# The results of attention kept in four tiles instead of one, and the temporaries of the first key and value chunks put into memory that is not yet in use

## The chip, the cores and the metric

The kernel runs on one core of a Trainium2 chip. A core has a matrix engine (PE; PEld is its weight load), three engines for elementwise work (DVE, ACT, POOL) and a queue engine (SP) that issues all of this kernel's transfers. Each engine runs its instructions in the order in which they stand in its queue, and waits on semaphores for the others. The metric is the time of one execution in microseconds (us) on the device, as the median of several runs: 1191.7 us before the change (1190.87 to 1192.7, three runs).

## The reference

One layer of a decoder, for a prompt of 1024 tokens and for 8 sequences of 8 new tokens each ("sample" tokens, 64 in all, kept as tile 8 beside the prompt's tiles 0 to 7 of 128 tokens). All in float32, model width 1024.

```
mixer:  h = LN0(x)*(1+scale1)+shift1 ; [q|k|v|zu|zv] = h @ w_in
        group A: chunked causal spatial gating unit  u * (tril(W_s) v + b_s)
        group B: sliding-window (128) GQA with per-head sinks, partial rotary
        x = LN1(alpha*x + gate1 * concat(A, B) @ w_o)
ffn:    h = LN0(x)*(1+scale2)+shift2 ; x = LN2(alpha*x + gate2 * SwiGLU(h))
```

Group B has 8 query heads of width 64, which share 2 key and value heads. Keys and queries are rotated (the first 16 of 64 features), and a block of 128 queries sees its own and the previous block of keys. The outputs are both token sets, the new key and value windows, and the normalised v rows of the gating unit.

## The kernel before, in words

Products of float32 are made as three products of split operands (high times high, low times high, high times low), so every weight is loaded as a raw tile and split: ACT copies the high part (`load_unit`, L104) and DVE subtracts it for the low part (L105). The pair is called a unit; units go into the four places of the pool `wts` or into places of a pool that the caller names.

The stages of the mixer, in the program's order:

1. Normalisation and the u and zv projections (token-major products, L212 for prompt tiles and L216 for tile 8), with the gating unit's small products (L408), which DVE multiplies into the u tiles (L414). The u tiles are stored to a scratch tensor (L419).
2. Projections of keys, values and queries (`project`, L496), in three chunks of tokens: c = 0 and 1 of 384, c = 2 of 320. A key or query chunk is then rotated (`rotate`): DVE shuffles it out of PSUM into `sh` (L505), ACT copies it into `z` (L506), POOL does three elementwise operations on them (`pool_tt`, L109). The rotated keys are copied and split into `KS` (L531 to L536). A value chunk is copied into `v32` (L548), transposed (L552) and split into `VS`. Products of this stage go into the two PSUM banks of tag a (the third key chunk into one of tag c), so a new chunk waits until DVE and ACT have read the one two before it.
3. Attention: for each pair of query heads t = 0 to 3 and each pair of token blocks, scores (L627), softmax (L596 to L614, for part of the blocks on POOL, L109 `s<-s,den`), transposes (L643), copies and splits of these (L645, L646), the product with values (L651), and the sum of its two halves by DVE into `stash` (L655, L657). For t = 3 the pairs go in the order (6,7), (0,1), (2,3), (4,5). After each of these `split_attention` splits two tiles of `stash` into the operand of the output projection (ACT L449, DVE L450). Attention of the sample tokens (`attend_sample`) lies between, with the cached keys and values `KC` and `VC`.
4. The output projection with units `wo[0]` to `wo[7]`, 128 rows of `w_o` each. `wo[4]` to `wo[7]` (the gating unit's rows) are made during attention in `wts`; `wo[0]` to `wo[3]` (attention's rows) after it, in the pool `w3`. `out_group(2)` does tiles 6, 7 and 8 (48 products L212 with `wo[0]` to `wo[3]` for tiles 6 and 7, whose other half `mix_part` has made earlier and stored, and 32 products L216 for tile 8), into all banks of tags a, b and d. `out_tile` then does tiles 0 to 5, 48 products each, in the banks a and b by turns. `prep_tile` brings the gating unit's results (load `mt`, transposes L458, L461, L462). `merge_tile` and `norm_tile` add the residual and normalise; for tiles 6 and 7 POOL does part of it (L109 `r<-r,g1p` and `r<-r,xt`), before which DVE can't read the bank (L838).
5. The feed-forward part: features (`ffn_features`, L880 to L906), which are stored and loaded again, and then a long run of products that keeps PE busy.

The order on each engine is not that of the source. The framework schedules the whole program when it is built, and decides by modelled times and by what waits for what, memory included: a tile that takes the memory of an earlier one waits for the last users of that one (`reuse_waits="tile"`: of the tiles that overlap it). So a change of places moves instructions.

The places on the right side of memory, in KiB per partition from the right end: `xb` 24 (it holds the x tiles at first, then rotation tables `rc` and `rs`, `KC`, `VC`, masks, the sample queries `QZ`, attention's half sum `o2s`), then `stash` 16. When both pools close, the same places go to `XF` (6) and then to the four units of `w3` (8 each, at 6 to 38), so these lie over `xb` and over `stash`. `sh` and `z` are tiles of the pool `rt` on the left side, in places that stage 1 used.

```
stash = stp.tile([P, 4, SEQ], F32, name="stash")
w3 = w3_ctx.enter_context(tc.tile_pool(name="w3", bufs=4, side="right", reuse_waits="tile"))
```

Of the kernel before, what the change touches and what calls it, by code (L numbers as in the profile page):

```python
# [10 lines left out]
F32 = mybir.dt.float32  # L11
# [6 lines left out]
P = 128  # L18
D = 1024
KD = D // P  # L20
SEQ = 1024
NS = 64
NTOK = SEQ + NS
# [22 lines left out]
def tile_block(  # L46
# [8 lines left out]
    nc = tc.nc  # L55
# [169 lines left out]
    st_ctx = ExitStack()  # L225
    xbp = st_ctx.enter_context(tc.tile_pool(name="xb", bufs=1, side="right"))
    xb = xbp.tile([P, 6 * D], F32, name="xb")

    offs = np.cumsum([0, NTOK, NTOK, 8 * P, 8 * P, 3 * P, 384, 512, 512, P])
    rc, rs, KC, VC, msk, msks, QZ, o2s, kvo = [xb[:, offs[n] : offs[n + 1]] for n in range(9)]  # L230
# [7 lines left out]
    with ExitStack() as p1:  # L238
# [8 lines left out]
        xt = [xb[:, i * D : (i + 1) * D] for i in range(6)]  # L247
# [124 lines left out]
        nc.sync.dma_start(out=KC, in_=kc_t)  # L372
        nc.sync.dma_start(out=VC, in_=vc_t)
# [68 lines left out]
    stp = st_ctx.enter_context(tc.tile_pool(name="stash", bufs=1, side="right", reuse_waits="tile"))  # L442
    stash = stp.tile([P, 4, SEQ], F32, name="stash")
    def split_attention(i):
        rows = rows_of(i)
        c, off = tok_cols(i)
        hi, lo = mix_dst(i, 0)
        sv = stash[:, :, i * P : i * P + rows] if i < 8 else ssm
        nc.scalar.activation(out=hi, in_=sv, func=AF.Copy)  # L449
        nc.vector.tensor_tensor(out=lo, in0=sv, in1=hi.bitcast(F32), op=ALU.subtract)  # L450
# [13 lines left out]
    with ExitStack() as p2:  # L464
# [22 lines left out]
        nc.gpsimd.memset(QZ, 0.0)  # L487

# [11 lines left out]
        def rotate(pt, c):  # L500
            n = CW[c]
            t0 = 384 * c
            sh = rt.tile([P, 384], F32, tag="sh", name="sh")
            z = rt.tile([P, 384], F32, tag="z", name="z")
# [18 lines left out]
        for c in range(3):  # L523
            z = rotate(project(units[0], c, "aac"[c]), c)
# [18 lines left out]

        units.append(load_unit(w_qkv[4]))
        for c in range(3):
            pt = project(units[1], c)
            v32 = rt.tile([P, 384], F32, tag="z", name="v32")
# [16 lines left out]

        units.append(load_unit(w_qkv[5]))
# [51 lines left out]
        def attend(t, bs):  # L617
# [38 lines left out]
            for h in range(2):  # L656
                nc.vector.tensor_tensor(  # L657
                    out=stash[64 * h : 64 * h + 64, t, bs[0] * P : (bs[0] + 2) * P].rearrange("p (b q) -> p b q", q=P),
# [48 lines left out]
        def load_wo(k, pool=None):  # L707
            wo[k] = load_unit(w_o[k * P : (k + 1) * P, :], pool)
# [64 lines left out]
    with ExitStack() as p3:  # L773
        w3_ctx = p3.enter_context(ExitStack())
        w3 = w3_ctx.enter_context(tc.tile_pool(name="w3", bufs=4, side="right", reuse_waits="tile"))
# [5 lines left out]
        for k in range(4):  # L781
            load_wo(k, w3)
# [761 lines left out]
```

## Time and profile before

| what | value |
|---|---|
| runs before | 1192.7, 1191.7, 1190.87 us; median 1191.7 us |
| the profiled execution | 1190.98 us, its span on the core 1189.2 us |
| busy share of the span | PE 95%, PEld 77%, DVE 67%, ACT 42%, POOL 14% |
| granted PE clock, mean | 0.979 of full speed |
| bytes moved | 204.96 MB, mean 172 GB/s |

A row of a timeline names the start and the length of a group, the engine, the line, output and inputs with their sizes, and in square brackets how long the engine stood idle before it and what ended that. Rows of matmuls have modelled ends. A row of a table by stretches has, for each stretch of the span, busy time and count of instructions per engine, the mean granted PE clock, and the share and rate of the transfers.

### The profile page before, as it was taken

The numbers are of one execution on the slowest core, as the hardware profiler recorded it, in microseconds if no ns is written. First come the engines' busy times: TensorE is split into PE (matmuls) and PEld (weight loads), VectorE is DVE, ScalarE is ACT, GpSimd is POOL, SyncE is SP. The second block draws the span as 40 slices with busy tenths as digits, with TensorE's granted clock in tenths as the row PEclk, the third lists the DMA queues.
The fourth block names the chain that finished last, engine by engine and source line by source line (L and its number), as shares of the span: only waits on it lengthen the run. The fifth ranks groups of instructions, "written<-read, shape, count | busy, mean of one in ns | idle before, by whom it ended". The sixth has DMA issues, their size and how long they took to land.

```text
span 1189.2 us, 16244 instructions
## 1 busy us (share of the span) xinstructions
PE 1126.9 (95%) x5845; PEld 914.7 (77%) x5845; DVE 801.2 (67%) x1460; ACT 505.3 (42%) x920; POOL 171.1 (14%) x173
## 2 busy tenths in 40 slices
PE   4999998999979999799999999999999999999997
PEld 2676688887758877477888888888888888788885
DVE  4434355898776979568487467467467565879786
ACT  3553124675761255545444434434433454343200
POOL 2212434654135111000000000000000000000021
PEclk9999998999989999799999999999999999999999
DMA  9935344122353424554545515515514488957951
GB/s 330 296 109 188 96 148 154 56 76 94 107 194 119 152 100 168 181 175 139 202 161 195 203 47 193 204 54 186 203 52 170 151 313 290 336 193 258 325 204 71
DMA packets 96352, 204.96 MB, mean 172 GB/s; under 512 B 10304, under 2 KB 32704, under 8 KB 96256
## 3 DMA queue, kind: packets, MB, share of 16 engines
q1 hardware_dynamic: 96272, 203.92, 49.6%
q8 instruction: 46, 0.75, 0.3%
q14 instruction: 34, 0.28, 0.1%
HBM read 149.43 MB, written 55.44 MB: 172 GB/s over the span
## 4 chain that ended last, share of the span: by engine, by line
PE 76%; DVE 10%; DMA 7%; ACT 3%; issue 2%; SPq 1%; POOL 1%; DVEq 0%; ACTq 0%; POOLq 0%
PE ps_a L967 17%; PE ps_b L967 13%; PE ps_a L212 11%; PE ps_b L212 4%; PE ps_c L973 3%; PE ps_a L1243 3%; PE ps_b L1243 3%; PE ps_c L1243 3%; PE ps_d L1243 3%; DMA g<-g_d 2%; PE ps_a L496 2%; DMA rwd<-in_w_down 1%; PE ps_d L364 1%; DVE s L614 1%; DVE bn L115 1%
## 5 line engine op out<-in xcount | busy, mean ns | idle before, releaser
L967 PE MATMUL ps_a<-H,wgu 128*128 128x512 f32 x560 | 160.1, 390 | 1.3 <-ACT wgu L956 1.3
L967 PEld LDWEIGHTS ps_a<-H,wgu 128*128 128x128 f32 x560 | 105.1, 188 | 23.7 <-ACT wgu L956 1.7
L957 DVE TENSOR_TENSOR wgu<-rawgu,wgu 128x1024 fp32r<-128x1024 f32 x79 | 96.2, 1220 | 33.1 <-ACT wgu L956 33.0
L1280 POOL TENSOR_TENSOR rstd<-ve,neghalf 128x1 f32<-128x1 f32 (+1 forms) x9 | 13.6, 1513 | 695.1 <-DVE ve L1278 695.1
L212 PE MATMUL ps_a<-unit,XA 128*128 128x512 f32 x384 | 103.9, 413 | 6.5 <-ACT unit L104 4.7
L956 ACT ACTIVATE wgu<-rawgu 128x1024 fp32r<-128x1024 f32 x79 | 82.0, 1055 | 58.4 <-PE ps_a L967 48.0
L967 PE MATMUL ps_b<-H,wgu 128*128 128x512 f32 x320 | 104.1, 390 | 0.0
L967 PE MATMUL ps_b<-XA,wgu 128*128 128x512 f32 x344 | 96.6, 396 | 0.0
L212 PEld LDWEIGHTS ps_a<-unit,XA 128*128 128x128 f32 x384 | 73.2, 196 | 28.0 <-ACT unit L104 4.9
L873 DVE TENSOR_TENSOR tpo<-tpr,tpo 128x512 fp32r<-128x512 f32 x77 | 50.9, 686 | 60.6 <-ACT tpo L872 60.6
L967 PEld LDWEIGHTS ps_b<-XA,wgu 128*128 128x128 f32 x344 | 65.0, 191 | 13.2
L872 ACT ACTIVATE tpo<-tpr 128x512 fp32r<-128x512 f32 x77 | 45.1, 625 | 66.8 <-DMA tpr<-in_w_down 32.5
L967 PEld LDWEIGHTS ps_b<-H,wgu 128*128 128x128 f32 x320 | 60.0, 188 | 12.7 <-ACT H L872 0.5
L967 PE MATMUL ps_a<-XB,wgu 128*128 128x512 f32 x160 | 62.4, 390 | 0.0
L961 DVE TENSOR_TENSOR rawgu<-rawgu 128x1024 f32<-128x1024 f32 x44 | 53.3, 1211 | 12.4 <-DMA rawgu<-in_w_gu 12.4
L1243 PE MATMUL ps_a<-opnd 128*128 128x512 f32 x198 | 57.9, 391 | 3.2 <-ACT opnd L1220 3.2
L967 PE MATMUL ps_a<-XA,wgu 128*128 128x512 f32 x240 | 59.8, 392 | 0.0
L1243 PE MATMUL ps_b<-opnd 128*128 128x512 f32 x198 | 57.6, 389 | 0.0
L1243 PE MATMUL ps_c<-opnd 128*128 128x512 f32 x198 | 57.4, 389 | 0.0
L1243 PE MATMUL ps_d<-opnd 128*128 128x512 f32 x198 | 57.2, 389 | 0.0
L496 PE MATMUL ps_a<-XA,unit 128*128 128x384 f32 (+1 forms) x264 | 51.5, 342 | 4.8 <-ACT z L506 3.3
L967 PEld LDWEIGHTS ps_a<-XA,wgu 128*128 128x128 f32 x240 | 44.3, 188 | 8.8
(361 smaller groups left out, 2355.9 us busy)
## 6 DMA issues: line engine op xcount, KB each, us to landing
rawgu<-in_w_gu SPq DMA_DIRECT2D x44, 512.0 KB
t_d<-tpo SPq DMA_DIRECT2D x44, 512.0 KB
opnd<-t_d SPq DMA_DIRECT2D x33, 512.0 KB
tpr<-in_w_down SPq DMA_DIRECT2D x22, 512.0 KB
g<-g_d SPq DMA_DIRECT2D x44, 256.0 KB
u<-in_w_ada SPq DMA_DIRECT2D x32, 256.0 KB
raw<-in_w_ada SPq DMA_DIRECT2D x16, 512.0 KB
raw<-in_w_ada SPq DMA_DIRECT2D x32, 256.0 KB
```

What stands on the lines that cost most here:

```text
L115: nc.vector.bn_stats(out=bn[:rows, h, :], in_=src[:, 512 * h : 512 * (h + 1)])
L212: mm(out=pt, lhsT=X[c][:, xp, k, off : off + P], rhs=rhs_of(units, k, wp), start=st and q == 0, stop=sp and q == 2)
L496: mm(out=pt[:, :n], lhsT=w[:, wp, k * P : (k + 1) * P], rhs=X[c][:, xp, k, :], start=(k == 0 and q == 0), stop=(k == KD - 1 and q == 2))
L872: nc.scalar.activation(out=hi, in_=src, func=AF.Copy)
L873: nc.vector.tensor_tensor(out=lo, in0=src, in1=hi.bitcast(F32), op=ALU.subtract)
L956: nc.scalar.activation(out=w[:, 0], in_=r, func=AF.Copy)
L957: nc.vector.tensor_tensor(out=w[:, 1], in0=r, in1=w[:, 0].bitcast(F32), op=ALU.subtract)
L961: nc.vector.tensor_tensor(out=out, in0=in0, in1=in1, op=op)
L967: mm(out=banks[m], lhsT=w[:, wp, m, k * P : (k + 1) * P], rhs=b[xp][:, k, :], start=first and k == 0 and q == 0, stop=last and k == 3 and ...
L973: mm(out=pt[:, 256 * half : 256 * half + 256], lhsT=XF[:, k0 + k, :], rhs=w[:, wp, :, k * P : (k + 1) * P], start=first and k == 0 and wp ...
L1243: mm(out=banks[tb], lhsT=st[sp][:, tb * P : (tb + 1) * P], rhs=mv[wp], start=first and q == 0, stop=last and q == 2, skip_group_check=True)
L1280: nc.gpsimd.tensor_tensor(out=rstd[:rows], in0=ve[:rows], in1=neghalf[:rows], op=ALU.pow)
```

## The change

It has two parts, and both only say where tiles lie.

- `stash` becomes four tiles, one for each pair of token blocks, each in a pool of its own. From the right end the places are now: `xc` 4 (a new tile for `QZ` and `o2s`), `xb` 20, a pool `sh` with two places of 1.5 for the tile `sh`, then `stash3` (tiles 6 and 7), `stash0`, `stash1`, `stash2`, 4 each. The four units of `w3` are four pools of one place each at the same 8 KiB steps from 6 on. So `wo[0]` and `wo[1]` lie over `xb`, `wo[2]` over the end of `xb`, over `sh` and over the first part of `stash3`, and `wo[3]` over the rest of `stash3`, `stash0` and most of `stash1`.
- `sh` and `z` of key chunks 0 and 1 are put into `KC` and `VC`, and `v32` of value chunks 0 and 1 into `o2s` and `QZ` (the list `early`). For that the loads of `KC` and `VC` are issued after the key chunks in the source, and the zeroing of `QZ` after the value chunks.

The list of instructions on every engine is the same as before, with other tiles; only the order differs.

```diff
+    xcp = st_ctx.enter_context(tc.tile_pool(name="xc", bufs=1, side="right"))
     xbp = st_ctx.enter_context(tc.tile_pool(name="xb", bufs=1, side="right"))
-    xb = xbp.tile([P, 6 * D], F32, name="xb")
-
-    offs = np.cumsum([0, NTOK, NTOK, 8 * P, 8 * P, 3 * P, 384, 512, 512, P])
-    rc, rs, KC, VC, msk, msks, QZ, o2s, kvo = [xb[:, offs[n] : offs[n + 1]] for n in range(9)]
+    xc = xcp.tile([P, D], F32, name="xc")
+    xb = xbp.tile([P, 5 * D], F32, name="xb")
+
+    offs = np.cumsum([0, NTOK, NTOK, 8 * P, 8 * P, 3 * P, 384, P])
+    rc, rs, KC, VC, msk, msks, kvo = [xb[:, offs[n] : offs[n + 1]] for n in range(7)]
+    QZ, o2s = xc[:, 0:512], xc[:, 512:1024]
+    early = [t[:, o : o + 384] for t in (KC, VC) for o in (0, 512)] + [o2s[:, 0:384], QZ[:, 0:384]]
...
-        xt = [xb[:, i * D : (i + 1) * D] for i in range(6)]
+        xt = [xb[:, i * D : (i + 1) * D] for i in range(5)] + [xc]
...
-        nc.sync.dma_start(out=KC, in_=kc_t)
-        nc.sync.dma_start(out=VC, in_=vc_t)
...
-    stp = st_ctx.enter_context(tc.tile_pool(name="stash", bufs=1, side="right", reuse_waits="tile"))
-    stash = stp.tile([P, 4, SEQ], F32, name="stash")
+    shp = st_ctx.enter_context(tc.tile_pool(name="sh", bufs=2, side="right", reuse_waits="tile"))
+    stash = {}
+    for n in (3, 0, 1, 2):
+        stp = st_ctx.enter_context(tc.tile_pool(name=f"stash{n}", bufs=1, side="right", reuse_waits="tile"))
+        stash[n] = stp.tile([P, 4, 2 * P], F32, name=f"stash{n}")
+
     def split_attention(i):
...
-        sv = stash[:, :, i * P : i * P + rows] if i < 8 else ssm
+        sv = stash[i // 2][:, :, (i % 2) * P : (i % 2 + 1) * P] if i < 8 else ssm
...
-        nc.gpsimd.memset(QZ, 0.0)
-
...
-        def rotate(pt, c):
+        def rotate(pt, c, own=None):
...
-            sh = rt.tile([P, 384], F32, tag="sh", name="sh")
-            z = rt.tile([P, 384], F32, tag="z", name="z")
+            sh, z = own or [q.tile([P, 384], F32, tag=g, name=g) for q, g in ((shp, "sh"), (rt, "z"))]
...
         for c in range(3):
-            z = rotate(project(units[0], c, "aac"[c]), c)
+            z = rotate(project(units[0], c, "aac"[c]), c, early[2 * c : 2 * c + 2] if c < 2 else None)
...
+        nc.sync.dma_start(out=KC, in_=kc_t)
+        nc.sync.dma_start(out=VC, in_=vc_t)
         units.append(load_unit(w_qkv[4]))
         for c in range(3):
             pt = project(units[1], c)
-            v32 = rt.tile([P, 384], F32, tag="z", name="v32")
+            v32 = early[4 + c] if c < 2 else rt.tile([P, 384], F32, tag="z", name="v32")
...
+        nc.gpsimd.memset(QZ, 0.0)
         units.append(load_unit(w_qkv[5]))
...
-                    out=stash[64 * h : 64 * h + 64, t, bs[0] * P : (bs[0] + 2) * P].rearrange("p (b q) -> p b q", q=P),
+                    out=stash[bs[0] // 2][64 * h : 64 * h + 64, t, :].rearrange("p (b q) -> p b q", q=P),
...
-        w3 = w3_ctx.enter_context(tc.tile_pool(name="w3", bufs=4, side="right", reuse_waits="tile"))
+        w3 = [
+            w3_ctx.enter_context(tc.tile_pool(name=f"w3{n}", bufs=1, side="right", reuse_waits="tile"))
+            for n in range(4)
+        ]
...
-            load_wo(k, w3)
+            load_wo(k, w3[k])
```

How it moves instructions, at the places of which the prediction speaks. Line numbers in rows of the changed kernel are those of its own source, up to 9 higher.

PE where the projections of keys end and those of values begin. `ps_a<-XA,unit 128x384` and `ps_c<-XA,unit 128x320` up to the row with x5 are keys, the next `128x384 x24` is the first value chunk; `ps_b<-gvt,wst` are the gating unit's products. Before:

```order
L496 MATMUL ps_c<-XA,unit 128x320 x15
L408 MATMUL ps_b<-gvt,wst 128x256 x2
L496 MATMUL ps_c<-XA,unit 128x320 x2
L408 MATMUL ps_b<-gvt,wst 128x256 x10
L496 MATMUL ps_c<-XA,unit 128x320 x5
L408 MATMUL ps_b<-gvt,wst 128x256 x12
L496 MATMUL ps_a<-XA,unit 128x384 x24
L496 MATMUL ps_a<-XB,unit 128x384 x24
L496 MATMUL ps_a<-XA,unit 128x320 x16
L515 MATMUL ps_c<-ident,z 128x128
```

Now:

```order
L500 MATMUL ps_c<-XA,unit 128x320 x5
L500 MATMUL ps_a<-XA,unit 128x384 x18
L410 MATMUL ps_b<-gvt,wst 128x256 x12
L500 MATMUL ps_a<-XA,unit 128x384 x6
L500 MATMUL ps_a<-XB,unit 128x384 x24
L500 MATMUL ps_a<-XA,unit 128x320 x24
L500 MATMUL ps_a<-XA,unit 128x384 x24
L500 MATMUL ps_a<-XB,unit 128x384 x12
L518 MATMUL ps_c<-ident,z 128x128
```

18 products of the first value chunk now stand ahead of the gating unit's last 12, and all three value chunks and one and a half query chunks ahead of the first transpose that needs the third key chunk's `z`.

PE at the end of attention (L643 transposes, L651 products with values, L212 output projection, L151 a small product of the conditioning, L458 transposes of `mt`). Before:

```order
L651 MATMUL ps_d<-pT,VS 128x256 x8
L643 MATMUL ps_c<-ident,s 128x128 x4
L651 MATMUL ps_d<-pT,VS 128x256 x5
L643 MATMUL ps_c<-ident,s 128x128 x4
L651 MATMUL ps_d<-pT,VS 128x256 x3
L643 MATMUL ps_c<-ident,s 128x128 x4
L651 MATMUL ps_d<-pT,VS 128x256 x8
L212 MATMUL ps_a<-unit,XA 128x512 x4
L212 MATMUL ps_b<-unit,XA 128x512 x4
L458 MATMUL ps_c<-ident,mt 128x64 x4
```

Now (L657 is the product with values, L649 the transposes):

```order
L649 MATMUL ps_c<-ident,s 128x128 x4
L212 MATMUL ps_a<-unit,XA 128x512 x2
L212 MATMUL ps_b<-unit,XA 128x512 x2
L657 MATMUL ps_d<-pT,VS 128x256
L212 MATMUL ps_a<-unit,XA 128x512 x10
L212 MATMUL ps_b<-unit,XA 128x512 x10
L657 MATMUL ps_d<-pT,VS 128x256 x4
L212 MATMUL ps_a<-unit,XA 128x512 x4
L212 MATMUL ps_b<-unit,XA 128x512
L649 MATMUL ps_c<-ident,s 128x128
L657 MATMUL ps_d<-pT,VS 128x256 x3
L649 MATMUL ps_c<-ident,s 128x128 x7
```

After these come 7 more products L212, the last 8 products with values, the last 12 products L212, transposes of `mt`, and tile 8's 32 products L216. So 36 of the 48 products of tiles 6 and 7 now stand ahead of attention's last product; none did.

DVE at the same place (L105 low part of a unit, L450 low part of an attention tile, L646 split of transposes, L657 sum into `stash`, L610 and L611 denominators of the last pair's softmax). Before:

```order
L610 TENSOR_TENSOR den<-den,es 128x4
L160 TENSOR_TENSOR mod_95<-mod_95,bada 128x64 x2
L450 TENSOR_TENSOR XA<-stash,XA 128x4x128
L611 RECIPROCAL den<-den 128x4
L163 TENSOR_SCALAR mod_95<-mod_95 128x64
L450 TENSOR_TENSOR XA<-stash,XA 128x4x128
L646 TENSOR_TENSOR pT<-ps_c,pT 128x512
```

Now (L616 and L617 denominators, L456 the attention tile, L652 the transposes):

```order
L160 TENSOR_TENSOR mod_95<-mod_95,bada 128x64 x2
L163 TENSOR_SCALAR mod_95<-mod_95 128x64
L105 TENSOR_TENSOR unit<-raw,unit 128x1024 x2
L616 TENSOR_TENSOR den<-den,es 128x4
L456 TENSOR_TENSOR XA<-stash_1483,XA 128x4x128 x2
L652 TENSOR_TENSOR pT<-ps_c,pT 128x512
L617 RECIPROCAL den<-den 128x4
```

The low parts of `wo[0]` and `wo[1]` now stand ahead of the last pair's denominators, and those of `wo[2]` and `wo[3]` further down in the same tail; before, all four stood behind the last attention tile. On ACT the high parts moved in the same way: those of `wo[0]` and `wo[1]` stand ahead of the last exponential of the sinks (L609). On SP the loads of `wo[2]`, `wo[3]` and of one feed-forward weight now stand ahead of `g1p` and of what follows it (`mt`, x tiles, `p_d`).

## The prediction, made before the changed kernel ran

> **What bounds the kernel now.** I read the page's busy shares and its chain of waits first, then a table by stretches, then the timeline of the stretches where PE is not full.
>
> ```profile
> PE 1126.9 (95%) x5845; PEld 914.7 (77%) x5845; DVE 801.2 (67%) x1460; ACT 505.3 (42%) x920; POOL 171.1 (14%) x173
> PE 76%; DVE 10%; DMA 7%; ACT 3%; issue 2%; SPq 1%; POOL 1%; DVEq 0%; ACTq 0%; POOLq 0%
> ```
>
> PE sets the time: it is busy 95% of the span and holds 76% of the chain that ended last. So an edit is worth the PE idle time that it closes, and the time that the clock is below 1.00 around such a hole. The table gives both for the stretches that the change touches (after each stretch its length; then busy time of PE, PEld, DVE, ACT, POOL with counts; granted clock; DMA share; GB/s):
>
> ```profile
> 177.88:181.14 3.26, 0.00 (x0) 0.00 (x0) 3.12 (x8) 0.54 (x2) 0.50 (x1) 0.90 0.31 99
> 181.14:192.60 11.46, 11.43 (x48) 11.11 (x48) 5.97 (x12) 5.00 (x10) 8.30 (x9) 0.73 0.78 276
> 192.60:194.10 1.50, 0.00 (x1) 0.00 (x1) 1.03 (x2) 0.52 (x2) 0.42 (x1) 1.00 0.55 192
> 194.10:215.00 20.90, 20.90 (x134) 20.76 (x135) 9.47 (x18) 10.92 (x23) 9.75 (x9) 1.00 0.14 44
> 215.00:340.00 125.00, 116.99 (x975) 98.80 (x973) 107.89 (x353) 85.01 (x251) 53.56 (x58) 0.98 0.29 93
> 338.00:346.73 8.73, 7.34 (x44) 5.71 (x36) 8.17 (x20) 5.77 (x10) 2.41 (x2) 0.83 0.50 154
> 346.73:351.43 4.70, 0.00 (x1) 0.01 (x1) 3.16 (x7) 3.16 (x6) 0.00 (x0) 0.61 0.68 219
> 351.43:372.90 21.47, 21.47 (x92) 17.11 (x93) 10.53 (x10) 6.02 (x8) 11.05 (x5) 0.93 0.51 191
> 372.90:447.60 74.70, 74.70 (x347) 59.84 (x346) 65.01 (x130) 25.54 (x44) 15.62 (x15) 1.00 0.37 122
> ```
>
> There are two places. Between 177.88 and 194.10 PE stands still twice, and runs at 0.73 between the two. At the end of attention it stands still for 4.70 us, with clocks of 0.83 and 0.93 on either side. From 372.90 to 447.60 (tiles 0 to 5) PE is never idle, so what is won ahead of that moves it earlier one for one.
>
> **Part A, the first key and value chunks.** The timeline shows the first hole and its cause:
>
> ```profile
> 170.15 2.17 POOL L109 TENSOR_TENSOR g<-g,lnb 128x512 f32<-128x512 f32 x1
> 179.13 0.87 DVE L414 SCALAR_TENSOR_TENSOR u<-ps_b,bst,u 128x256 f32<-128x256 f32 x2
> 179.93 0.58 DVE L505 STREAM_SHUFFLE sh<-ps_a 128x384 f32<-128x384 f32 x1
> 180.64 1.96 POOL L109 TENSOR_TENSOR sh<-sh,xb 128x384 f32<-128x384 f32 x2 [8.32 <-issue]
> 181.14 7.27 PE L496 MATMUL ps_a<-XA,unit 128*128 128x384 f32 x24 [3.27 <-ACT z L506]
> 185.51 0.52 ACT L531 ACTIVATE KS<-z 64x384 fp32r<-64x384 f32 x1 [3.99 <-POOL z L109]
> 186.47 0.17 DVE L482 TENSOR_SCALAR nsnk<-snk 128x8 f32<-128x8 f32 x1 [5.48 <-DMA snk<-in_sinks]
> 194.10 2.61 PE L496 MATMUL ps_a<-XA,unit 128*128 128x320 f32 x16 [1.52 <-ACT v L548]
> 210.81 0.64 PE L627 MATMUL ps_b<-KS,qs 128*128 128x256 f32 x4
> ```
>
> The shuffle of the first key chunk out of its bank (L505) comes only at 179.93, behind the last products into u (L414), though POOL had nothing to do since 170.15 + 2.17 = 172.32. The first value chunk needs that bank, so PE waits 3.27 for the copy L506. The second hole, 1.52, is the third value chunk's wait for the copy of the first (L548). With `sh`, `z` and `v32` of chunks 0 and 1 in idle memory, L505 and L506 depend on nothing but the key chunk's products.
>
> The bound from above: both holes close, 3.26 + 1.50, and the stretch between them runs at full clock instead of 0.73, 11.46 x 0.27 = 3.09. The sum is 7.9 us. That the clock comes back with the hole is my reading of the table, where it falls next to holes; the second hole, with 1.00 on both sides, speaks against it, and without it A is 4.8. Can what follows arrive that early? POOL starts its rotations at about 172.3 instead of 180.64, so its chain is 8.3 ahead, enough for 7.9. The first scores, L627 at 210.81, would start at about 203. The bound from below: the last L414s are now behind 18 value products at 7.27/24 = 0.30 each, some 5 us of PE work, which itself starts earlier. By my walk they end 3 us later than without those products. The gating unit's stores and the load of `snk` follow them on SP, so the denominators' L482 may come 2.5 us after its 186.47. DVE waits there, with the subtractions of KS behind it. These can't start before the first copy L531 anyway, which still waits for POOL's first rotations and, on ACT, for two L548. If all of it fell on the path, 2.5 would go off, and A would be 2.3 at the least. I take 7.9, since three full banks of queued products stand on PE ahead of the first use of KS.
>
> The zeroing of `QZ` moves into POOL's rotations, and the loads of `KC` and `VC` move behind the key chunks:
>
> ```profile
> L487 POOL MEMSET xb<- x1: 530/530/530, 69.5 to 69.5; 128x512 f32 x1
> L666 PE MATMUL ps_b<-xb x32: 269/273/297, 263.3 to 312.4; 128*32 128x128 f32 x32
> ```
>
> The first costs POOL 0.53 us, ahead of the second query chunk, and is covered by PE's queued query products; uncovered it would cost 0.53. The loads are first used at 263.3, some 60 us after they are issued: zero.
>
> Between the two places, 215 to 340, PE is busy 116.99 of 125 and DVE 107.89. Neither swallows a shift by itself, as every instruction there moves along with its producers. I count zero change of length.
>
> **Part B, units of the output projection one by one.** The hole at the end of attention:
>
> ```profile
> 336.24 0.19 ACT L609 ACTIVATE es<-es 128x4 f32<-128x4 f32 x1
> 340.04 2.41 POOL L109 TENSOR_TENSOR s<-s,den 128x512 f32<-128x512 f32 x2 [4.33 <-DVE mod L163]
> 346.11 0.62 PE L651 MATMUL ps_d<-pT,VS 128*128 128x256 f32 x3 [0.74 <-DVE pT L646]
> 348.99 1.29 DVE L450 TENSOR_TENSOR XB<-stash,XB 128x512 fp32r<-128x512 f32 x2 [0.24 <-ACT XB L449]
> 350.32 2.00 ACT L104 ACTIVATE unit<-raw 128x1024 fp32r<-128x1024 f32 x2 [0.84 <-DVE XB L450]
> 351.43 2.08 PE L212 MATMUL ps_a<-unit,XA 128*128 128x512 f32 x4 [4.70 <-ACT unit L104]
> 353.83 2.39 POOL L109 TENSOR_TENSOR r<-r,g1p 128x1024 f32<-128x1024 f32 x1 [11.38 <-DMA xt<-in_x]
> 359.46 5.78 PE L216 MATMUL ps_d<-unit,XS 128*128 128x512 f32 x24
> 361.32 4.42 DVE L105 TENSOR_TENSOR unit<-raw,unit 128x1024 fp32r<-128x1024 f32 x2 [0.26 <-ACT unit L104]
> 369.99 1.33 DVE L838 TENSOR_TENSOR xt<-ps_a,g1p 128x512 f32<-128x512 f32 x2 [4.24 <-issue]
> 372.90 11.31 PE L212 MATMUL ps_a<-unit,XA 128*128 128x512 f32 x48
> L105 DVE TENSOR_TENSOR unit<-raw,unit x19: 1211/1225/3287, 18.6 to 364.5; 128x1024 fp32r<-128x1024 f32 x19
> ```
>
> The first unit is made at 350.32, behind the last split of `stash` (L450), and PE waits 4.70 for it. From above: PE without any gap or slow clock from 338.00 to 372.90 would save 4.70, then 8.73 − 7.34 = 1.39 and 7.34 x 0.17 = 1.25, then 21.47 x 0.07 = 1.50: 8.8 us.
>
> That isn't reached, since the new instructions stand ahead of attention's last softmax. In the times of before: L104 for `wo[0]` and `wo[1]` run on ACT from 336.3 to 338.4, and L609 moves 2.2 us, from 336.24 to 338.5. On DVE the conditioning's L163 (its end let POOL start at 340.04) moves up to 339.2, as small steps now stand behind it; two L105 at 1.22 then end at 341.6; the two splits L450 (1.29), a split of transposes and the denominators end at 344, and POOL's `s<-s,den` starts then instead of 340.04. It ends at 346.4, where it ended at 342.45. PE has work meanwhile: the first 24 products L212 take 24 x 11.31/48 = 5.7 us, to about 349 with what stands between. Then follow 12 more products, the last transposes and the last products with values, each step with ACT and DVE between. I get 356.2 for attention's end on PE, where it was 346.73: 9.5 later, of which 36 x 0.236 = 8.5 is work taken over from behind. Behind it lie 12 products (2.8), transposes of `mt` with their copies (2.2) and the 32 products L216 (32 x 5.78/24 = 7.7), which gives 369.2 for the first product of tile 0. A second chain ends beside it: the x tiles' loads land 353.83 − 346.73 = 7.1 after attention's end, so at 363.3, POOL needs 2 x 2.39 to 368.1, and L838's 1.33 frees the bank at 369.4. So tile 0 starts at 369.5 where it started at 372.90: **B = 3.4 us**, between 0 (both chains as late as before) and 8.8.
>
> On SP the loads of `wo[2]`, `wo[3]` and one feed-forward weight now stand ahead of `g1p`, `mt` and the x tiles. The last of them waits until `wo[2]` is split, which is ahead of attention's last products; so the 7.1 holds. If it waited longer, the second chain would be late by as much; that is the part of the range toward 0.
>
> One rule speaks against B. The Trainium skill ("SBUF — State Buffer", section "Who interferes with whom") says that a VectorE instruction with two SBUF inputs and a GpSimd instruction that reads SBUF shut each other out for their whole length. The trace agrees: two L105 took 4.42 us at 361.32 beside POOL's row of 2.40, against a median of 1.225 each. By it the L105s in the tail could meet POOL's 2.41 and cost up to that, with B at 1.0 and the time at 1182.8. Against it stands the order: the first two L105s precede the denominators for which POOL waits.
>
> **The sum.** A 7.9 + B 3.4 = 11.3. The profiled execution took 1190.98 (span 1189.2 and 1.8 around it): 1190.98 − 11.3 = 1179.7. The median of runs lies 0.7 above it, which gives 1180.4, rounded to **1180**. Two later places have their order changed a little, the start of the feed-forward features above all. There PE is not full, so I allow 3 us either way:
>
> ```profile
> 460.00:550.00 90.00, 76.90 (x310) 58.01 (x309) 63.78 (x94) 47.36 (x75) 1.97 (x3) 0.87 0.46 153
> ```
>
> **The rivals.**
> - *Only A counts.* The wait for places at the end of attention goes, but attention ends later by as much as the projection starts earlier. For it: the 8.5 us of inserted products and the x loads that come only after attention's end. Against: PE's 4.70 and the slow clocks are real losses. 1191.7 − 7.9 = 1184.
> - *Only B counts.* DVE, busy 107.89 of 125 in attention, is so nearly the bound that the earlier start is lost on the way. Against: its work moves with PE's. 1191.7 − 3.4 = 1188.
> - *Slower.* Blocks of products ahead of attention's small steps starve DVE, which later is short of time:
>
> ```profile
> 292.95 6.45 PE L212 MATMUL ps_a<-unit,XA 128*128 128x512 f32 x20
> 299.55 0.45 DVE L691 COPY ssm<-ps_c 64x64 f32<-64x64 f32 x2 [5.68 <-PE ps_c L687]
> ```
>
>   A block of 20 let DVE idle 5.68. The new order has unbroken blocks of 19, 22 and 20 between scores and values, where before there was one of 20 and three up to 10. If the two more each cost 5.68, that is 11.4, B's gain is never made, and A gives back 7.9: 1191.7 + 3.5 = 1195. It decides once the two cost over 7.9 + 2.4 together. Against: PE is busy during such a block, so only what DVE can't make up is lost.
> - *No difference.* A is swallowed as in the second rival and the x loads eat B: 1191.7. What the diff says about places is plain in the order, so that it does nothing at all is unlikely.
>
> **How the numbers follow.** About 0.2%, 2.4 us, is what a measurement can tell from no change. Forecast 0.53, with its own range 1174 (both upper bounds, 16.7, and rounded out) to 1183; only A 0.19; only B 0.08; slower 0.13; no difference 0.07. Faster is 0.53 + 0.19 + 0.08 = 0.80. The range for 8 in 10 goes from 1171 (both bounds and 3 us at the features) to 1190, and leaves out the slower case and most of no difference.
>
> **What would show it.** In the profile of the changed kernel: no PE idle time between 172 and 195 and a clock near 1.00 there; POOL's 8.32 ahead of its first rotation gone; first L627 near 203; the first product of tile 0 near 372.9 − 11.3 = 361.6. PE's 4.70 for L104 gone, and attention's last product with values some 9.5 later than its start would have it. A is wrong if the stretch from the first scores to attention's end is longer by more than those 9.5; B is wrong if PE stands still behind attention's last product for `mt` or a bank.

## The result, and the profile after

The changed kernel takes 1185.78 us (median of six runs, 1183.19 to 1187.37), the kernel before 1192.2 on the same chip (six runs). The ratio is 0.9942, 95% interval 0.9926 to 0.9958: **6 to 7 us faster**, where 1180 was forecast and 11.3 us of gain. That is outside the forecast's own range (1174 to 1183) and inside the range for 8 in 10 (1171 to 1190). The profiled execution took 1184.28 with a span of 1182.5; that of before has a span of 1189.2, so the two traces differ by 6.7.

Six starts on PE cut the span into stretches. They are read from PE's timelines; the last column reaches to the span's end.

| stretch, us | before | after | difference |
|---|---|---|---|
| start to first key product | 163.1 | 162.7 | −0.4 |
| to the first scores (part A) | 47.8 | 39.2 | **−8.6** |
| to the last scores (attention) | 121.5 | 126.5 | **+5.0** |
| to the first product of tile 0 (part B) | 40.6 | 35.7 | **−4.9** |
| to the first feed-forward product | 74.7 | 74.5 | −0.2 |
| to the first product with reloaded features | 54.4 | 57.7 | **+3.3** |
| to the end | 687.2 | 686.3 | −0.9 |

Both parts did what they were meant to do, and rather more. Of the 13.5 us that they won, 8.3 were given back, at two places where the forecast put zero. The stretches of the changed kernel, in the columns of the prediction's table by stretches:

```profile
162.65:201.80 39.15, 39.15 (x248) 39.02 (x247) 23.72 (x46) 16.40 (x31) 19.13 (x17) 1.00 0.55 195
201.80:328.30 126.50, 116.33 (x947) 99.35 (x946) 110.64 (x340) 84.12 (x245) 54.49 (x60) 0.99 0.24 79
328.30:364.00 35.70, 30.79 (x181) 24.07 (x180) 23.07 (x45) 19.52 (x39) 10.97 (x7) 0.95 0.67 218
438.50:496.20 57.70, 45.13 (x199) 34.13 (x197) 40.05 (x64) 31.98 (x56) 4.50 (x5) 0.80 0.48 167
```

and attention before, which the prediction's table cut elsewhere:

```profile
210.80:332.30 121.50, 115.20 (x943) 98.56 (x942) 105.19 (x338) 83.45 (x240) 55.65 (x59) 0.99 0.25 81
```

From the first key product to the first scores PE is now busy without a gap and at a clock of 1.00. In attention PE's busy time grew by 1.1, but DVE's by 5.45, for two instructions more (splits of `VS`, 1.0 us in all, which stood ahead of the first scores before). That is about the length that attention gained. The granted clock isn't the reason, since it is 0.99 in this stretch in both. What PE waits for there (columns: us in all, times, longest), before and after:

```profile
PE ps_b L627 <- DVE nm L596: 1.0, 1, 1.0
```

```profile
PE ps_b L633 <- DVE nm L602: 5.0, 4, 2.0
PE ps_b L672 <- DVE nm L602: 1.5, 1, 1.5
```

`nm` is the maximum of a block of scores, which DVE takes before the bank is free for the next scores. PE now waits 6.5 us for it, where it waited 1.0.

The timeline of the end of attention, after:

```profile
332.23 1.99 ACT L104 ACTIVATE unit<-raw 128x1024 fp32r<-128x1024 f32 x2
334.57 2.36 DVE L105 TENSOR_TENSOR unit<-raw,unit 128x1024 fp32r<-128x1024 f32 x2
339.06 2.04 POOL L109 TENSOR_TENSOR s<-s,den 128x512 f32<-128x512 f32 x2 [7.37 <-DVE den L617]
340.79 1.38 DVE L105 TENSOR_TENSOR unit<-raw,unit 128x1024 fp32r<-128x1024 f32 x1 [0.44 <-ACT unit L104]
346.91 1.32 PE L657 MATMUL ps_d<-pT,VS 128*128 128x256 f32 x8
350.23 1.74 PE L212 MATMUL ps_a<-unit,XA 128*128 128x512 f32 x4 [2.00 <-ACT unit L104]
356.16 7.65 PE L216 MATMUL ps_d<-unit,XS 128*128 128x512 f32 x32 [0.34 <-DVE XS L468]
357.02 2.41 POOL L109 TENSOR_TENSOR r<-r,g1p 128x1024 f32<-128x1024 f32 x1 [15.93 <-DMA xt<-in_x]
361.96 1.29 DVE L847 TENSOR_TENSOR xt<-ps_a,g1p 128x512 f32<-128x512 f32 x2 [4.79 <-POOL r L109]
364.00 11.32 PE L212 MATMUL ps_a<-unit,XA 128*128 128x512 f32 x48
```

The first two units are made at 332, ahead of the last softmax. PE's wait of 4.70 for a unit has become one of 2.00 for the last unit, and tile 0 starts at 364.00 instead of 372.90. As in the walk of the prediction two chains end there together: PE's 32 products for tile 8 at 363.8, and x landing at 357.02, two POOL operations and L847 at 363.2.

### The profile page after: what moved, and what is told of

It is laid out like the page before. It is cut to its first block, busy times and chain, and to the rows that moved or that the text cites. A ratio compares the mean times of both kernels' runs of the same rounds, so it can differ in the third digit from the quotient of the medians.

```text
span 1182.5 us, 16229 instructions
## 1 busy us (share of the span) xinstructions
PE 1122.4 (95%) x5845; PEld 911.0 (77%) x5845; DVE 805.0 (68%) x1460; ACT 504.3 (43%) x920; POOL 171.8 (15%) x173
## 4 chain that ended last, share of the span: by engine, by line
PE 49%; DMA 6%; DVE 2%; ACT 1%; issue 1%; SPq 1%; DVEq 0%; ACTq 0%
PE ps_a L976 17%; PE ps_b L976 12%; PE ps_c L982 3%; PE ps_a L1252 3%; PE ps_c L1252 3%; PE ps_b L1252 3%; PE ps_d L1252 3%; DMA g<-g_d 2%; DMA rwd<-in_w_down 1%; DMA hb<-h_d 1%; PE ps_c L976 1%; PE ps_c L1157 1%; PE ps_d L1157 1%; DVE hb L970 1%; PE ps_d L1413 1%
## 5 line engine op out<-in xcount | busy, mean ns | idle before, releaser
L1289 POOL TENSOR_TENSOR rstd<-ve,neghalf 128x1 f32<-128x1 f32 (+1 forms) x9 | 13.6, 1511 | 694.6 <-DVE ve L1287 694.6
L212 PE MATMUL ps_a<-unit,XA 128*128 128x512 f32 x384 | 102.7, 409 | 4.3 <-ACT unit L104 2.0
L212 PEld LDWEIGHTS ps_a<-unit,XA 128*128 128x128 f32 x384 | 72.5, 195 | 25.2 <-issue 2.5
L121 POOL TENSOR_TENSOR rstd<-ve,neghalf 128x1 f32<-128x1 f32 (+1 forms) x36 | 31.0, 862 | 143.7 <-DVE ve L119 143.3
```

The source lines that it names most:

```text
L121: nc.gpsimd.tensor_tensor(out=rstd[:rows], in0=ve[:rows], in1=neghalf[:rows], op=ALU.pow)
L212: mm(out=pt, lhsT=X[c][:, xp, k, off : off + P], rhs=rhs_of(units, k, wp), start=st and q == 0, stop=sp and q == 2)
L1289: nc.gpsimd.tensor_tensor(out=rstd[:rows], in0=ve[:rows], in1=neghalf[:rows], op=ALU.pow)
```

## The experiments

All ratios are against the kernel before, timed on the same chip beside it.

| run | what | ratio (95%) | first to last scores, us | DVE busy in it, us |
|---|---|---|---|---|
| before | | 1 | 121.5 | 105.2 |
| after | both parts | 0.9942 (0.9926 to 0.9958) | 126.5 | 110.6 |
| 1 | A alone | 0.9944 (0.9925 to 0.9963) | 127.9 | 110.6 |
| 2 | B alone | 0.9966 (0.9951 to 0.9981) | 121.4 | 104.9 |
| 3 | after, no split for t = 0 | 0.9852 (0.9832 to 0.9872) | 120.8 | 105.0 |
| 4 | before, no split for t = 0 | 1.0003 (0.9989 to 1.0017) | 124.2 | 105.7 |
| 5 | before, two units early | 1.0006 (0.9993 to 1.0018) | 125.2 | 106.2 |
| 6 | after, two sums on POOL | 0.9952 (0.9937 to 0.9967) | 130.1 | 111.7 |
| 7 | after, no rotation for t = 1 | 0.9868 (0.9849 to 0.9886) | 120.9 | 106.0 |
| 8 | after, half of t = 1 on POOL | 0.9944 (0.9930 to 0.9958) | 127.1 | 108.3 |
| 9 | after, 8 on ACT | 0.9902 (0.9882 to 0.9921) | 124.4 | 107.4 |
| 10 | before, 8 on ACT | 1.0019 (1.0005 to 1.0033) | 129.0 | 108.6 |
| 11 | after, 16 on ACT | **0.9827** (0.9807 to 0.9846) | 119.3 | 102.6 |
| 12 | before, 16 on ACT | 0.9977 (0.9965 to 0.9989) | 124.2 | 103.3 |

The last two columns are of one profiled execution each. In the rows where the clock of that stretch is 0.99 (before, after, 3, 7 and 11) the length is DVE's busy time plus 14.9 to 16.7; in the others, at 0.95 to 0.97, plus 16.5 to 20.9. Run 6 has the changed kernel's order there and takes 3.6 longer, at a clock of 0.95, so a difference of that size between two rows can be the clock's.

### Which part wins what: A alone, B alone

A alone is the kernel before with

```diff
+    early = [t[:, o : o + 384] for t in (KC, VC) for o in (0, 512)] + [o2s[:, 0:384], QZ[:, 0:384]]
...
+            sh, z = own or [rt.tile([P, 384], F32, tag=g, name=g) for g in ("sh", "z")]
...
+            v32 = early[4 + c] if c < 2 else rt.tile([P, 384], F32, tag="z", name="v32")
```

and the loads of KC and VC and the zeroing of QZ moved as in the change. B alone is the changed kernel without these.

> The kernel before with part A alone (sh, z and v32 of chunks 0 and 1 in idle memory; stash, xb and w3 as before). Theory 1, attention has no room on DVE and eats about half of A's head start whatever the tail looks like: first scores 9 us earlier than before (near 202), last scores only 4 earlier (near 328), tile 0 of the output projection 4 earlier (near 369), time about 1188. Theory 2, the 5 us are lost because of B's order: first and last scores both 9 earlier, tile 0 near 364, time about 1183.

> The changed kernel with A undone (key and value temporaries in rt again, KC, VC and the zeroing of QZ where they were). Theory 1: first and last scores as before (near 211 and 332), tile 0 about 5 earlier (near 368), time about 1188, and the two parts' gains add up to that of both. Theory 2: B costs up to 5 in attention and wins it back behind it, so tile 0 near 373 and time about 1192.

A alone took 1187.37 (before 1194.17). Its first scores come 39.2 us after the first key product, as with both parts, and its attention takes 127.9. So the loss in attention comes with A and needs nothing of B (PE's waits for `nm` are 4.9 and 1.5 there, as after the change): theory 2 falls. B alone took 1189.84. Its attention takes 121.4, and the stretch from the last scores to tile 0 takes 35.8, as after the change; so the 4.9 of the tail are B's, with or without A. By the ratios A is worth 6.7 and B 4.1, 10.8 together, and both at once 6.9. This difference of 3.9 is at the edge of what the intervals, some 2 us either way on each, can tell. One thing is plain in them: A alone (0.9944) is as fast as both parts (0.9942). On top of A, B gains nothing that could be measured; the profiles show its tail 4.8 shorter than run 1's (40.6 and 35.8) and the stretch of the feed-forward features, below, 4.6 longer (53.1 and 57.7).

The gain of A at its own place may be larger than 8.6: from the first key product to the first scores the six kernels without A take 47.8 to 51.3 us (before, 2, 4, 5, 10, 12), of which before is the shortest, and all eight with A take 39.2.

B alone also shows what the separate pool for `sh` does by itself. It doesn't open the start, which takes 51.3 us: the wait for the first key chunk's copy shrinks from 3.27 to 0.58, and that for the first value chunk's grows from 1.52 to 8.08.

```profile
177.68 4.45 PE L504 MATMUL ps_a<-XA,unit 128*128 128x384 f32 x24 [0.58 <-ACT z L513]
194.38 1.97 PE L504 MATMUL ps_a<-XA,unit 128*128 128x320 f32 x6 [8.08 <-ACT v L555]
```

What the tail gives is taken back, in part or whole, where the feed-forward features are made. From the first feed-forward product to the first with reloaded features the kernels without B take 53.1 to 54.4 us (before, 1, 4, 10, 12), all with B 55.9 to 57.7 (after, 2, 3, 6, 7, 8, 9, 11).

### Is it DVE? Less work for it in both kernels

```diff
-                nc.vector.tensor_tensor(out=pT[:, 1], in0=pp, in1=pT[:, 0].bitcast(F32), op=ALU.subtract)
+                if t > 0:
+                    nc.vector.tensor_tensor(out=pT[:, 1], in0=pp, in1=pT[:, 0].bitcast(F32), op=ALU.subtract)
...
-                           rhs=pT[:, q, 256 * kb : 256 * kb + 256], ...
+                           rhs=pT[:, q if t > 0 else 0, 256 * kb : 256 * kb + 256], ...
```

> The changed kernel, but for the first pair of heads (t = 0) the split of the transposed scores is left out: DVE's low part L652 isn't made, 8 times 0.69 = 5.5 us less on DVE between 220 and 245, and PE multiplies the high part twice, so PE's work is the same and the output is not the reference's. Theory 1 (DVE is what holds attention up once A has given it an early start): last scores 4 to 5 us earlier than in the changed kernel, time about 1181. Rival (PE sets the pace there, DVE's idle time is spread): at most 1 us.

> The same omission in the kernel before. Theory 1: before the change PE was itself nearly full while t = 0 ran (19.84 us busy of 20 from 229 to 249), so less DVE work wins 1 to 2 us, time about 1190. Rival (DVE sets the pace of attention in both kernels alike): the same 4 to 5 us as in the changed kernel, time about 1187. Rival (PE sets it in both): 0 to 1 us, 1191.

After: 1177.16, 10 us below the 1187 that 0.9942 makes of the kernel before's 1194.17 beside it, and attention back at 120.8. Before: no difference. So DVE's 5.5 us counted in full once A had moved the start, as theory 1 had it. The gain in time is larger than it gave, and only half of it is in the profiles, whose spans differ by 5.2 (1182.5 and 1177.3). For the kernel before the run proves less than it seems to. DVE's busy time in attention didn't fall there (105.7 against 105.2), although 5.5 us of splits are gone, because other instructions got longer: the normalisation `s<-s,den` of the softmax went from a mean of 563 ns to 591, and the denominators and low parts grew too. So run 3 shows that relief for DVE shortens attention in the changed kernel; what relief would win without A this run doesn't show. Leaving work out also moves the order of attention's instructions in both kernels, and run 4's attention had a clock of 0.95.

### Two units alone, and two sums on POOL

Run 5 is the kernel before with `QZ` and `o2s` in a tile of their own and `w3` in four pools, and with one `stash`:

> The kernel before with QZ and o2s in a tile of their own and the four units of w3 in four pools, but one stash and no part A: wo[0] and wo[1] are made early, wo[2] and wo[3] still behind the last split of stash, 24 products stand ahead of attention's last product instead of 36. If B's gain of 5 us in the tail comes from the first two units alone: tile 0 about 4 to 5 earlier than before, time about 1190 or a little less, as with B whole. If the split of stash carries half of it: tile 0 2 to 3 earlier, time about 1192. If the loss of 2 to 3 us at the start of the feed-forward part belongs to all that makes tile 0 start earlier, it is there here too, in the measure of tile 0's gain.

1193.48 against 1192.85: no gain. Its tail takes 39.5 instead of 40.6, less than a quarter of B's 4.9. 24 products stand ahead of attention's last product, as expected, but PE's wait of 4.70 is still there, now for the third unit:

```profile
361.86 2.07 PE L212 MATMUL ps_a<-unit,XA 128*128 128x512 f32 x4 [4.70 <-ACT unit L104]
```

So it is the split of `stash`, which lets `wo[2]` and `wo[3]` come early too, that carries B; the second reading was right in that, and even too high. (Its attention of 125.2 had a clock of 0.95.) The third reading asked where the loss at the features comes from. That stretch takes 56.0 here, as long as in the kernels with B, although the tail gains only 1.1. So the loss doesn't grow with the tail's gain; it seems to go with the places that run 5 shares with B, as far as one profile of run 5 tells.

Run 6 was aimed at the loss in the features:

```diff
-        vtt(r11, r11, r21, ALU.subtract)
-        vtt(r21, r21, r22, ALU.add)
+        tt = pool_tt if p == 0 else vtt
+        tt(r11, r11, r21, ALU.subtract)
+        tt(r21, r21, r22, ALU.add)
```

> The changed kernel, with the two sums of the first four feed-forward weights (L970, 2 times 1.2 us on DVE between 440 and 465) on POOL, where they take about 2.4 each; nothing else moves but a few rows there. Theory: from the last product of tile 5 to the last normalised tile DVE is the bound (23.6 us busy of 25.7), so the transposes there start up to 2.4 earlier and the time falls by 1 to 2, to about 1184. Rival: the sums are needed in time by the products and POOL is too slow for it, or the POOL's powers of the normalisation queue behind them: same or up to 2 slower.

1186.93, ratio 0.9952: no gain, within the interval of the change's own 0.9942. The stretch takes 56.3 instead of 57.7. The two operations took 6.95 us on POOL, and a DVE instruction beside them 2.90 instead of 1.22:

```profile
445.36 6.95 POOL L109 TENSOR_TENSOR rawgu<-rawgu 128x1024 f32<-128x1024 f32 x2 [4.54 <-DMA rawgu<-in_w_gu]
450.49 2.90 DVE L966 TENSOR_TENSOR wgu<-rawgu,wgu 128x1024 fp32r<-128x1024 f32 x1 [0.31 <-ACT wgu L965]
```

So the run doesn't say whether DVE is the bound there, since what it took off the list it gave back by stretching. Why the stretch is some 2 to 3 us longer with B stays open. What the profile shows is a chain through DVE, ACT, stores and reloads, in which PE waits for the last normalised tile and for the copies of the features.

### What made DVE's time grow

The list of DVE is the same; its instructions got longer. Two groups between the first and the last scores, before and after (count, busy us, mean ns):

```profile
L614 DVE TENSOR_SCALAR s<-s,den 128x256 f32<-128x256 f32 x40 | 20.3, 563 | 0.1
L601 DVE TENSOR_TENSOR es<-nm,snk 128x4 f32<-128x4 f32 x15 | 3.5, 234 | 0.2
```

```profile
L620 DVE TENSOR_SCALAR s<-s,den 128x256 f32<-128x256 f32 x40 | 24.1, 657 | 0.3
L607 DVE TENSOR_TENSOR es<-nm,snk 128x4 f32<-128x4 f32 x15 | 6.0, 402 | 0.1
```

After the change the same normalisation `s<-s,den` takes between 340 and 1164 ns. Four in a row beside a POOL at work (after), and four with POOL idle (before):

```profile
238.71 1.01 POOL L109 TENSOR_TENSOR sh<-sh,xb 128x384 f32<-128x384 f32 x1 [4.69 <-DVE mod L163]
238.85 3.38 DVE L620 TENSOR_SCALAR s<-s,den 128x256 f32<-128x256 f32 x4
239.68 1.05 POOL L109 TENSOR_TENSOR z<-z,xb 128x384 f32<-128x384 f32 x1
240.81 1.01 POOL L109 TENSOR_TENSOR z<-z,sh 128x384 f32<-128x384 f32 x1
```

```profile
232.58 1.21 POOL L578 TENSOR_TENSOR qs<-z,qs 64x384 fp32r<-64x384 f32 x1 [3.07 <-issue]
235.25 1.13 DVE L614 TENSOR_SCALAR s<-s,den 128x256 f32<-128x256 f32 x4
238.67 0.88 POOL L109 TENSOR_TENSOR sh<-sh,xb 128x320 f32<-128x320 f32 x1 [4.88 <-DVE sh L505]
```

3.38 us against 1.13. By the trace's starts and ends, the first three of the four beside POOL end 0.15 us after a POOL operation does, and the fourth, with POOL idle, takes 0.34. The Trainium skill ("SBUF — State Buffer", section "Who interferes with whom") names `tensor_scalar` among the operations that can hold, in a two-port mode, the ports shared with GpSimd, and says that who comes first blocks the other for a whole instruction; the trace agrees, with these numbers. The two groups grew by 3.8 and 2.5 us, the denominators' `den<-den,es` fell by 1.2, which makes 5.1 of the 5.45; the two splits of `VS` add 1.0, and the rest falls by 0.7 in sum.

The traces let one count the meetings. Of the 40 normalisations, 20 overlap a POOL operation before the change and 27 after it. In all fourteen profiles, those that no POOL operation overlaps take 334 to 357 ns; those that one overlaps take 762 to 943 in the mean and up to 1236. So the length of the group depends above all on how many of them meet POOL.

A run that keeps DVE's list and takes a part of POOL's away:

```diff
+            if not turn:
+                return z
             pool_tt(z[:, :n], z[:, :n], rc[:, t0 : t0 + n], ALU.mult)
...
-            z = rotate(project(w, c), c)
+            z = rotate(project(w, c), c, None, t != 1)
```

> The changed kernel, but the queries of t = 1 aren't rotated (9 POOL operations of about 1.05 us left out, z used as copied; the output is not the reference's). DVE's own list of work is the same. Theory collision: in attention DVE's instructions on two SBUF operands or one long one are stretched while POOL runs (s<-s,den 657 ns mean, median 372, most 1164, against 563 mean before the change), and that is what eats A: the mean falls to about 550, last scores 2 to 4 earlier, time about 1183. Theory amount of work: DVE's list is simply too long whatever POOL does: mean and time as in the changed kernel within 1 us.

1176.37, ratio 0.9868, nearly 9 us better than the changed kernel, where some 3 were expected; the mean of `s<-s,den` 617 (550 was expected), DVE busy 106.0 and attention 120.9. With DVE's list as it was, "simply too long whatever POOL does" falls. That the queries of t = 1 reach PE sooner without their rotation isn't it either: PE waits 0.4 us for POOL's `qs` in attention in both kernels, while its waits for `nm` fall from 6.5 to 1.5. In run 7:

```profile
PE ps_b L635 <- DVE nm L604: 1.5, 1, 1.5
PE ps_b L635 <- POOL qs L586: 0.4, 1, 0.4
```

The other way round, with more for POOL:

```diff
-            on_pool = (0, 0, 1, 2)[t]
+            on_pool = (0, 1, 1, 2)[t]
```

> The changed kernel with one of the two blocks of each softmax of t = 1 normalised on POOL instead of DVE (8 DVE instructions of 0.37 to 1.1 us go, 4 POOL instructions of 1.0 come). Theory amount of work: DVE has 3 to 5 us less in its fullest stretch, last scores 2 to 4 earlier, time about 1183. Theory collision: POOL's four more instructions stretch as many of DVE's by up to 0.8 each, so the gain is 0 to 1.

1186.01, ratio 0.9944, exactly the changed kernel's: eight DVE instructions fewer, those left at a mean of 684 (25 of 32 overlap POOL), as the collision theory has it.

### A place for it: ACT, in both kernels

```diff
+                if j >= act:
+                    nc.scalar.activation(out=so, in_=so, func=AF.Identity, scale=den[:, j : j + 1])
-                if j >= skip:
+                elif j >= skip:
...
-            den = softmax(jobs, snk[:, 2 * t : 2 * t + 2], 2 * on_pool)
+            den = softmax(jobs, snk[:, 2 * t : 2 * t + 2], 2 * on_pool, 2 if t < 2 else 4)
```

(with 3 in place of 2 in runs 9 and 10)

> The changed kernel, with the last of the four normalisations of each softmax of t = 0 and 1 on ACT (8 instructions, some 0.5 us each there) instead of DVE (0.66 us mean, stretched by POOL up to 1.16); all results are computed. If DVE's fullness in attention is what eats A: some 5 us less on DVE where it is full, last scores 3 to 5 us earlier, time about 1182. If not (ACT, on the same chain, is as much the limit): 0 to 1, time about 1186.

> The same move in the kernel before, as the control. If DVE holds up attention only once A has brought the start forward: 0 to 2 us, time about 1191, so that the two parts together are then worth 9 to 11 us between these two kernels, instead of 6 to 7. If DVE holds up both kernels alike: the same 3 to 5 as in the changed kernel, time about 1188.

> The changed kernel with two of the four normalisations of each softmax of t = 0 and 1 on ACT (16 instructions, 10 us less on DVE, 8 more on ACT, which is busy 12 to 15 of 20 us there). If DVE's room is what counts: 5 to 7 us faster than the changed kernel, time about 1180; if ACT becomes the next limit: no faster than with one of four.

> The kernel before with two of the four normalisations of each softmax of t = 0 and 1 on ACT, the control of the fastest version so far. In the runs so far attention's length, first to last scores, is DVE's busy time in it plus 15 to 17 us, whichever kernel, where the granted clock is 0.97 or more. By that theory this kernel gains in attention what DVE's busy time falls by (16 instructions fewer; 8 fewer gave nothing here, since those left were stretched to 775 ns): with some 6 us less, time about 1187, and the changed kernel's lead over it stays some 10 to 12 us. If DVE held up attention only after A: time as the kernel before, 1193 or so, lead 18 or more.

After the change 8 of them on ACT give 0.9902 (1182.87), as the first expectation had it, and 16 give **0.9827** (1174.87), more than expected: 20 us faster than the kernel before, some 11 (by the medians) to 14 (by the ratios) faster than the change, and the fastest of all. Attention takes 119.3, by the table of stretches and with the waits of PE in it, where the 6.5 us for `nm` have shrunk to 0.9:

```profile
202.90:322.20 119.30, 115.28 (x948) 99.79 (x947) 102.61 (x323) 90.42 (x262) 54.34 (x60) 0.99 0.27 84
```

```profile
PE ps_b L635 <- DVE nm L602: 0.9, 1, 0.9
```

The groups of the normalisation there, 24 left on DVE and 16 on ACT:

```profile
L622 DVE TENSOR_SCALAR s<-s,den 128x256 f32<-128x256 f32 x24 | 14.2, 633 | 0.3
L620 ACT ACTIVATE s<-s,den 128x256 f32<-128x256 f32 x16 | 7.2, 500 | 1.9 <-DVE den L617 1.9
```

On ACT they took 492 to 512 ns each in all four runs, whether POOL was at work or not (33 of the 48 overlap a POOL operation).

In the kernel before, 8 cost 0.19%, which neither reading of run 10 had foreseen, and 16 win 0.23% (0.11 to 0.35). The change's lead between the kernels with 16 on ACT is 1 − 0.9827/0.9977 = 1.5%, or 18 us (some 15 to 21 by the intervals), against 7 without, as the second reading of run 12 had it. So A and B are worth at least what they win at their own places once DVE has room. That DVE holds up attention only after A isn't shown by it, since DVE's busy time in run 12 is only 1.9 us below that of before. The expectation of run 12 by the sum "DVE's time plus 16" (−6 us) was too high. Its profiled execution was the slowest of its twelve (1199.59 against a median of 1192.83), so its row of the table is no typical one. Run 10 shows why this sum doesn't carry from kernel to kernel: 8 instructions fewer, and DVE is busier. Its group of the normalisation:

```profile
L616 DVE TENSOR_SCALAR s<-s,den 128x256 f32<-128x256 f32 x32 | 23.2, 775 | 0.2
```

Each new order puts other DVE instructions beside POOL's: 23 of these 32 overlap a POOL operation, against 20 of 40 before, and they cost more than the 40 did.

## Why the prediction was right or wrong

- **Part A** (7.9): right, 8.6 from the first key product to the first scores. Both holes and the low clock are gone, first scores at 201.8 (forecast near 203). That the clock comes back with the hole, which the prediction called its reading, came true (0.73 before, 1.00 after). `snk` came 1.5 later than before (its L488 at 187.94), and neither it nor the zeroing of `QZ` or the later loads cost anything that can be seen.
- **Attention, "zero change of length"**: this step failed. It took 5.0 more. The reason given, that every instruction moves along with its producers, holds for producers and consumers and forgot that POOL and DVE meet anew: DVE's 107.89 of 125 held instructions that POOL stretches (20 of 40 normalisations met POOL), and with A more of them did (27 of 40), which made them 4 to 5 us longer. Run 1 shows that A alone brings this, runs 3, 7 and 11 that relief for DVE takes it away. The prediction's own sign against A came out by this: from the first scores to attention's end it took 146.4 us instead of 135.9, 10.5 longer, where more than 9.5 was to mean that A is wrong. A's head start was there, and attention didn't keep it. The rival "only B counts" had the place and the engine, but as the loss of all of A; it was 5.0 of 8.6.
- **Part B** (3.4): right in kind, measured 4.9, and tile 0 at 364.0 where 361.6 was forecast, since attention brought 5.0 with it. Attention's last product came 5.5 later after the last scores (14.2 to 19.7), not 9.5. The walk had ACT, DVE and POOL one behind the other where they overlap more. The chain by the x tiles took 8.8 from attention's end to their landing, not 7.1. The loads ahead of it on SP did no more harm than that. (The walk's first chain adds up to 368.9, not 369.2; the second, at 369.4, decided the sum.)
- **The rule against B**: the L105s of `wo[0]` and `wo[1]` took 2.36 for two, and the third, while POOL ran, 1.38; the order kept them apart as said. DVE and POOL in each other's way decided the result after all, in attention, where the prediction hadn't placed it, although `s<-s,den` stands at a mean of 563 and a least of 339 ns in the trace of before.
- **The features, "zero, 3 either way"**: this step failed too, at the edge: +3.3. It comes with B, and it is there in run 5 with only part of B's places; its cause isn't settled.
- **The sum**: 8.6 − 5.0 + 4.9 − 3.3, with 0.4, 0.2 and 0.9 from the other stretches, is 6.7, where 11.3 was forecast. That the total stayed within the wide range is in part luck: losses of 8.3 that weren't forecast met a range that reached to "only A", and gains at A and B that were 2.2 above the forecast.
- **The rival "only A counts"**: its 1184 is nearest to the time that was measured, and A alone is in fact as fast as both parts. But its reason was another: the tail's gain is there, and it is lost at the features.
- **The rival "slower"**: its blocks of 19 and 22 products are there, but DVE's waits for the sample tokens' product behind such blocks fell, from 8.6 to 5.0 us.

## What to carry to other kernels

An idle hole that is closed pays in full only if the stage behind it isn't held by another engine; look at that engine's busy share in that stage, and then at the spread of single instructions, not at their count alone. The group whose mean stood well above its least time was stretched by a neighbour here, and each new order dealt these collisions out again. The cure was to take work from DVE to the engine whose time stayed the same beside POOL (ACT, 492 to 512 ns), not to POOL. And a control that takes work off an engine's list is one only if the engine's busy time falls.

## What the runs showed of the hardware that was not expected

- One DVE instruction of 128 x 256 took 334 to 357 ns alone and up to 1236 beside POOL; to give eight of them to POOL won nothing (run 8), to give sixteen to ACT at 500 ns each won 11 to 14 us (run 11).
- Runs 6 and after have the same order up to the features. On PE every score product up to 287 us comes 1.8 us later in run 6, which started that much later; behind 287 the distance is 3.3 and at the last scores 5.3. The two steps stand where the granted clock is lower in run 6 (the changed kernel first):

```profile
286.00:296.00 10.00, 8.86 (x45) 6.88 (x46) 6.58 (x18) 4.57 (x16) 5.08 (x5) 0.83 0.19 67
294.00:304.00 10.00, 10.00 (x101) 7.36 (x103) 6.75 (x18) 6.37 (x17) 1.93 (x2) 1.00 0.33 105
324.00:334.00 10.00, 8.24 (x107) 5.96 (x107) 7.67 (x26) 7.92 (x21) 3.38 (x4) 1.00 0.33 105
```

```profile
286.00:296.00 10.00, 7.60 (x39) 5.38 (x38) 7.11 (x21) 5.77 (x17) 5.21 (x4) 0.71 0.25 80
294.00:304.00 10.00, 10.00 (x76) 7.37 (x75) 5.45 (x17) 4.53 (x14) 1.07 (x1) 0.84 0.12 37
324.00:334.00 10.00, 8.68 (x73) 6.46 (x72) 6.17 (x26) 6.00 (x22) 2.44 (x3) 0.69 0.12 36
```

  So the spread between executions of one program (4.2 us over the six runs of the changed kernel) comes at least in part from where the clock dips, and a single profile's stretch lengths are known to no better than some 2 to 4 us.
